# Twenty output units of the third layer as Strassen pairs over both halves, computed ahead of the merge, and a table builder that holds its two tiles

## The chip, the cores and the metric

One core of a Trainium2 chip runs the whole program: three layers of a sequence model, one launch. The metric is device time in microseconds (us). Engines: PE does matmuls, ACT, DVE and POOL elementwise work, and SP issues most of the DMAs. Each engine executes its own list of instructions in a fixed order; an instruction that must wait holds up all that stand behind it on that engine.

## The reference

Input x is 1024 tokens of width 1024. Two layers of a mixer and a gated feed-forward network come first, then one block of two branches:

```
x = first_block(x, ...)        # two layers, each a mixer and a gated FFN
xn = rmsnorm_2(h, norm_pre_g[l])
proj = xn @ w_in[l]
u_a, z_a, o_a, i_a, f_a, u_b, z_b, g_pre = jnp.split(proj, split_points, axis=-1)
y_a = mlstm_branch(u_a, z_a, o_a, i_a, f_a, ...) @ w_a_out[l]
y_b = s5_branch(u_b, z_b, ...) @ w_b_out[l]
g = jax.nn.sigmoid(g_pre.astype(jnp.float32)).astype(h.dtype)
merged = g[..., :D_MODEL] * y_a + g[..., D_MODEL:] * y_b
h = h + rmsnorm_2(merged @ w_o[l], norm_post_g[l])
```

z_b is 512 wide and g_pre 2048. In output units of 128 columns of `w_in`, z_b is units 28 to 31, the first gate (g1) units 32 to 39, the second (g2) units 40 to 47. The state-space branch (s5) also needs tables of powers of its complex coefficients, which depend on weights alone.

## The kernel before

The tokens are two halves h of 512 columns. Activations lie as tiles of 128 x 512, eight for the model width. A product in 32-bit precision is made of three matmuls per k tile, since each operand is split into a high and a low part: high by high, high by low, low by high (`mm3`, L236 to L238). Weights come as tiles `raw` (SP, L175) and are split by ACT (L186) and DVE (L188) into `wsp`. The feed-forward up-products are already done by Strassen's scheme over a pair of output units and both halves (`quad`, L497): seven half-depth products take the place of eight, each of 12 matmuls. The first product of a pair can be computed earlier on half 0 alone (`ffn_first`) and kept in DRAM.

Tiles come from pools with fixed slots: `t4` (27 slots, a split tile of 128 x 2 x 512), `t2` (18 slots, 128 x 512), `raw` (3), `wsp` (8). A tile holds its slot until its last use; the first instruction on the next tile of that slot waits for it. A scheduler fixes the order of each engine in advance. Side work runs as generators, advanced a little at each group of matmuls (`start(generator, rate)`) and finished by `drain`.

Two places matter here. In layer 0's FFN, the down-product (`ffn_down`, L630 to L632, output `pd`) of half 0 has the s5 table builder (`s5_tables`) beside it. The builder makes 16 tables in eight rounds of two on POOL: clear a tile `s5R` (L1315, L1316), double the powers eight times (L1323 to L1328, with a scratch tile `s5rt`), and write both tables by DMAs that POOL issues (L1332). Then `hid_steps(1)` fetches the 22 tiles `hidd1_k` from DRAM into `xt` (SP, L260) and splits them into `hid` (ACT L246, DVE L250), which the down-product of half 1 needs in the order of k.

At the end of the third layer the merge of a half takes the s5 branch's output `y` (POOL `y5n` L1769, split into `y5s`), multiplies it by the glu weights (`pgl`), fetches the other branch's output `oar` (POOL `oa` L1781, DVE L1782), and multiplies both into `pya` and `pyb`. Units z_b (`pzb`, `merge_z`), g1 (`pg1`, `merge_g`) and g2 (`pg2`) are computed within and ahead of each merge; `proj_out` (`po`) and `finish` (norm and residual) follow.

Of the kernel before, what the change touches and what calls it, by code (L numbers as in the profile page):

```python
# [11 lines left out]
F32 = mybir.dt.float32  # L12
# [3 lines left out]
AF = mybir.ActivationFunctionType  # L16
ALU = mybir.AluOpType
# [32 lines left out]
class Weights:  # L50
# [13 lines left out]
    def part(self, k0):  # L64
        return Weights(self.parts, self.q, self.k0 + k0)


class Model:
# [20 lines left out]
    bg = ()  # L89
# [227 lines left out]
            self.nc.tensor.transpose(pb[:, 128 * b:128 * b + 128], r[:, b:b + 1].to_broadcast([128, 128]), self.ident)  # L317
        return pb

    def norm_steps(self, h, gname, gi, out):  # L320

        nc = self.nc
        pb = self.bcast(self.r[h])
        for k, t in enumerate(self.fetch(self.x[h][:NT])):
            nc.vector.scalar_tensor_tensor(t, t, self.col(gname, gi * NT + k), pb, ALU.mult, ALU.mult)
            out.append(self.split(t, "xs", low=nc.vector if k % 2 else nc.gpsimd))
            yield

# [904 lines left out]
    def s5_tables(self):  # L1233
        nc, io = self.nc, self.io
# [26 lines left out]
        cs, sn = sm("cs"), sm("sn")  # L1261
# [48 lines left out]
        V.tensor_tensor(t0, t0, t1, ALU.subtract)  # L1310
        V.tensor_tensor(qi, t0, den, ALU.mult)
        yield
        for g0 in range(0, 16, 2):
            R = self.t4("s5R", [128, 2, 2, 256], F32)
            G.memset(R[:, :, 0, 0:1], 1.0)  # L1315
            G.memset(R[:, :, 1, 0:1], 0.0)  # L1316
            tp = self.t2("s5rt", [128, 2, 2, 128])
            for k in range(8):
                n = 1 << k
                er, ei = (E[k][i][:, g0:g0 + 2].unsqueeze(2).to_broadcast([128, 2, n]) for i in range(2))  # L1320
                s, d = slice(0, n), slice(n, 2 * n)
                tm = (tp[:, 0, :, :n], tp[:, 1, :, :n])
                G.tensor_tensor(tm[0], R[:, :, 0, s], er, ALU.mult)  # L1323
                G.tensor_tensor(tm[1], R[:, :, 1, s], ei, ALU.mult)
                G.tensor_tensor(R[:, :, 0, d], tm[0], tm[1], ALU.subtract)
                G.tensor_tensor(tm[0], R[:, :, 0, s], ei, ALU.mult)
                G.tensor_tensor(tm[1], R[:, :, 1, s], er, ALU.mult)
                G.tensor_tensor(R[:, :, 1, d], tm[0], tm[1], ALU.add)  # L1328
                if k > 2:
                    yield  # L1330
            for i in range(2):
                G.dma_start(self.s5r[g0 + i], R[:, i])  # L1332
            yield
# [411 lines left out]
            nc.sync.dma_start(self.oad[h][:, k], hn[i])  # L1745
            yield

    def merge_z(self, xs):

        out = []  # L1750
        for c in range(2):
            for sp in self.wpair(self.io["w2_in"], 14 + c):
                ps = self.ps("pzb")
                self.mm3(ps, sp, xs, bg=1)
                z = self.t2("zb")
                self.nc.scalar.activation(z, ps, AF.Tanh, scale=0.5)
                self.nc.vector.scalar_tensor_tensor(z, z, 1.0, ps, ALU.add, ALU.mult)
                out.append(z)
                self.etick()
        return out  # L1760

    def merge_y(self, h):

# [19 lines left out]
            oa.append(t)  # L1783
        return oa

    def merge_g(self, xs, c, bg):

        out = []
        for sp in self.wpair(self.io["w2_in"], 16 + c):
            ps = self.ps("pg1")  # L1790
            self.mm3(ps, sp, xs, bg=bg)
            out.append(self.t2("g1"))
            self.nc.scalar.activation(out[-1], ps, AF.Tanh, scale=0.5)
        return out

    def merge(self, xs, h, zb, y, g1=()):

        nc, io = self.nc, self.io
        V = nc.vector
        yn, ys = y  # L1800
        if h:
            self.drain()
            oa = self.merge_oa(h)
        yb = []
        for c in range(2):
            for i, sp in enumerate(self.wpair(io["w2_glu"], c)):
                k = 2 * c + i
                pg = self.pa("pgl")
                self.mm3(pg, sp, ys, bg=1)
                t = self.t2("glu")  # L1810
                nc.scalar.activation(t, pg, AF.Tanh, scale=0.5, bias=self.hbglu[:, k:k + 1])
                V.scalar_tensor_tensor(t, t, 1.0, yn[k], ALU.add, ALU.mult)
                V.tensor_tensor(t, t, zb[k], ALU.mult)
                yb.append(self.split(t, "yb", 0.125))
                self.etick()
        if not h:
            oa = self.merge_oa(h)
        out = []
        for c in range(4):
            pr = g1 if g1 and not c else self.merge_g(xs, c, 0.5)  # L1820
            for t, sp in zip(pr, self.wpair(io["w2_ao"], c)):
                pa = self.ps("pya")
                self.mm3(pa, sp, oa, bg=0.5)
                V.scalar_tensor_tensor(t, t, 1.0, pa, ALU.add, ALU.mult)
            w2, wb = self.wpair(io["w2_in"], 20 + c), self.wpair(io["w2_bo"], c)
            for i in range(2):
                ps = self.ps("pg2")
                self.mm3(ps, w2[i], xs, bg=0.5)
                t = self.t2("g2")
                nc.scalar.activation(t, ps, AF.Tanh, scale=0.5)  # L1830
# [10 lines left out]
    def block2(self, xsA, norm, dst):  # L1841

        io = self.io
        xs = [xsA, []]
        self.s5_in(xs[0], 0)
        self.xs_store(xs[0], 0)
        st = self.mconv(xs[0], 0, 0)
        g = self.start(self.mgates(xs[0], 0))
        self.mout(xs[0], 0, st)
        self.finished()  # L1850
        nb = self.start(norm(xs[1]), 3.0)
        self.mz(xs[0], 0, st)
        self.drain(nb)
        self.s5_in(xs[1], 1)
        self.xs_store(xs[1], 1)
        self.drain(g)
        self.start(self.s5_main(), 2.2)
        a = b = ()
        for h in range(NH):
            for hd in range(4):  # L1860
                units = 2 * ("o" not in st) + 2 * ("z" not in st) + 2 * (hd < 3 or h == 0) + 4 * (hd == 3 and h == 1)
                self.drain(a)
                a, b = b, self.start(self.mattn(h, hd, st), self.TH / units)
                new = None
                if "o" not in st:
                    self.mout(xs[h], hd, st)
                if hd < 3:
                    new = self.mconv(xs[h], h, hd + 1)
                if "z" not in st:
                    self.mz(xs[h], hd, st)  # L1870
                if hd == 3 and h == 0:
                    xs[1] = self.xs_load(1)
                    g = self.start(self.mgates(xs[1], 1))
                    new = self.mconv(xs[1], 1, 0)
                    self.drain(g)
                if hd == 3 and h:
                    zb = self.merge_z(xs[1])
                    y = self.merge_y(1)
                    g1 = self.merge_g(xs[1], 0, 1)
                st = new  # L1880
        self.ahead = 90
        mg = self.merge(xs[1], 1, zb, y, g1)
        xs[0] = self.xs_load(0)
        m, ss = self.proj_out(io["w2_o"], mg)
        self.finish(1, m, ss, "norm_post_g_2", 0, dst=dst(1))
        y = self.merge_y(0)
        zb = self.merge_z(xs[0])
        mg = self.merge(xs[0], 0, zb, y)
        m, ss = self.proj_out(io["w2_o"], mg, last=True)
        self.finished()  # L1890
        self.finish(0, m, ss, "norm_post_g_2", 0, dst=dst(0), last=True)
        self.finished()

    def run(self, out):
# [4 lines left out]

        B, keep = [{}, {}], [[self.dp.tile([128, T], F32, name=f"keep{l}_{k}") for k in range(NT)] for l in range(2)]  # L1900
        self.hidd = [[self.dp.tile([128, T], F32, name=f"hidd{h}_{j}") for j in range(FFT)] for h in range(NH)]
        self.m1d = [self.dp.tile([128, T], F32, name=f"m1d{j}") for j in range(FFT)]

        def side():
# [3 lines left out]
            self.drain(nb)  # L1908
            self.ffn_first(0, FFT - 14, B[0], None)

        def hook(gname, gi):
            def steps():
                xs[0] = []
                yield from self.norm_steps(0, gname, gi, xs[0])
            return steps

        self.ahead = 90
# [23 lines left out]
            self.finish(h, *self.proj_out(io["od_out"], y[h]), "mix_post_g", 1, rate=0.5 if h == 0 else 1.25, pool=h == 1)  # L1941
        self.drain(nb)
        self.ahead = 90
        self.ffn(1, B[1], keep[1], ("ffn_pre_g", 1), hook("norm_pre_g_2", 0), (self.s5_tables2(), 2.6), 7)
        self.ahead = 90
        self.block2(xs[0], lambda o: self.norm_steps(1, "norm_pre_g_2", 0, o), part(out))


@with_exitstack
# [63 lines left out]
```

## Time and profile before

| what | value |
|---|---|
| median of 3 runs | 3246.97 us (3246.46 to 3247.01) |
| the profiled execution | 3246.84 us |
| its span, first to last instruction | 3245.1 us |
| mean granted clock of PE | 0.985 |
| PE busy | 3120.8 us (96%), 14320 matmuls |
| DVE busy | 2279.1 us (70%) |
| ACT busy | 1511.6 us (47%) |
| POOL busy | 784.9 us (24%) |

The terms of this document's sums refer to the profiled execution. The granted clock is a share of PE's full speed of 2.4 GHz: 0.50 is 1.2 GHz. Matmuls overlap one another, so the spacing of their starts, not the duration of one, is what a matmul costs.

### The profile page before, as it was taken

What the parts mean: (1) busy time and instruction counts of PE and PEld (TensorE: products, weight loads), DVE (VectorE), ACT (ScalarE), POOL (GpSimd) and SP (SyncE); (2) the same over time, 40 slices, a digit from 0 to 9 for tenths busy, and PEclk for the clock granted to TensorE, in tenths of its full rate; (3) what the DMA queues carried; (4) which work ended last, traced back from release to release, by engine and by line L of the source; (5) the groups of instructions that cost most, each with busy time, mean ns of one, the idle gap of its engine ahead of it and who ended that gap; (6) DMA issues with size and microseconds to landing.
All of it is one profiled execution on the core that took longest, in us unless ns stands there. A gap on an engine that the chain in (4) does not pass through costs nothing. (4 is left out here: it accounts for less than half of the span.)

```text
span 3245.1 us, 42204 instructions
## 1 busy us (share of the span) xinstructions
PE 3120.8 (96%) x14320; PEld 2546.8 (78%) x14320; DVE 2279.1 (70%) x4391; ACT 1511.6 (47%) x2804; POOL 784.9 (24%) x992
## 2 busy tenths in 40 slices
PE   8999998999996998999999999999999999999998
PEld 5777786888885787877788888778887878888886
DVE  7768758568873569597756887777687988743633
ACT  4646644433432457575433345545454445333332
POOL 4111104455459302022535530001010100100200
PEclk9999999999998999999999999999999999999999
DMA  4444445233443644346423355657544444434532
GB/s 153 160 133 141 140 141 174 85 109 129 155 158 115 213 129 133 91 139 225 152 82 129 126 174 169 215 190 242 173 133 167 128 146 143 132 95 149 179 101 95
DMA packets 206154, 474.07 MB, mean 146 GB/s; under 512 B 25705, under 2 KB 48425, under 8 KB 205937
## 3 DMA queue, kind: packets, MB, share of 16 engines
q1 hardware_dynamic: 204656, 467.18, 43.7%
q0 software_dynamic: 1280, 4.20, 0.3%
q8 instruction: 113, 1.85, 0.2%
q14 instruction: 105, 0.85, 0.1%
HBM read 367.86 MB, written 99.19 MB: 144 GB/s over the span
## 5 line engine op out<-in xcount | busy, mean ns | idle before, releaser
L188 DVE TENSOR_TENSOR wsp<-raw,wsp 128x512 fp32r<-128x512 f32 x890 | 651.6, 738 | 447.2 <-ACT wsp L186 442.6
L186 ACT ACTIVATE wsp<-raw 128x512 fp32r<-128x512 f32 x882 | 541.0, 617 | 819.7 <-PE pd L632 180.5
L630 PE MATMUL pd<-hid,wsp 128*128 128x512 f32 x704 | 279.6, 398 | 30.6 <-ACT hid L246 30.6
L631 PE MATMUL pd<-hid,wsp 128*128 128x512 f32 x704 | 279.1, 397 | 4.1 <-DVE hid L250 4.0
L632 PE MATMUL pd<-hid,wsp 128*128 128x512 f32 x704 | 278.6, 396 | 0.0
L630 PEld LDWEIGHTS pd<-hid,wsp 128*128 128x128 f32 x704 | 134.4, 191 | 59.6 <-ACT hid L246 32.2
L631 PEld LDWEIGHTS pd<-hid,wsp 128*128 128x128 f32 x704 | 134.2, 191 | 37.1 <-DVE hid L250 9.6
L492 PE MATMUL qy<-st,wsp 128*128 128x512 f32 x416 | 162.2, 390 | 0.5 <-ACT qm L502 0.5
L493 PE MATMUL qy<-st,wsp 128*128 128x512 f32 x416 | 161.9, 389 | 0.0
L494 PE MATMUL qy<-st,wsp 128*128 128x512 f32 x416 | 161.9, 389 | 0.0
L236 PE MATMUL pg<-xs,wsp 128*128 128x512 f32 x384 | 150.9, 393 | 10.6 <-DVE l1h L725 6.3
L632 PEld LDWEIGHTS pd<-hid,wsp 128*128 128x128 f32 x704 | 134.5, 191 | 27.1
L248 POOL TENSOR_TENSOR xs<-xt,xs 128x512 fp32r<-128x512 f32 x28 | 44.3, 1584 | 456.7 <-ACT xs L246 401.6
L238 PE MATMUL pg<-xs,wsp 128*128 128x512 f32 x384 | 150.1, 391 | 0.0
L237 PE MATMUL pg<-xs,wsp 128*128 128x512 f32 x384 | 150.0, 391 | 0.0
L524 POOL TENSOR_TENSOR qv<-qv,qu 128x512 f32<-128x512 f32 x44 | 69.9, 1589 | 287.4 <-ACT wsp L186 137.2
L186 ACT ACTIVATE wsp<-wss 128x512 fp32r<-128x512 f32 x88 | 55.6, 632 | 150.4 <-PE qy L494 66.4
L270 DVE TENSOR_TENSOR sq<-sq 128x512 f32<-128x512 f32 x140 | 98.4, 704 | 32.3 <-ACT sq L268 31.8
L188 DVE TENSOR_TENSOR wsp<-wss,wsp 128x512 fp32r<-128x512 f32 x88 | 79.8, 907 | 28.7 <-ACT wsp L186 26.7
L492 PE MATMUL pf<-xs,wsp 128*128 128x512 f32 x224 | 89.5, 400 | 7.8 <-DVE th L577 5.2
L236 PEld LDWEIGHTS pg<-xs,wsp 128*128 128x128 f32 x384 | 72.5, 189 | 27.4 <-ACT yo L246 6.7
L492 PEld LDWEIGHTS qy<-st,wsp 128*128 128x128 f32 x416 | 78.1, 188 | 17.9 <-ACT qm L502 0.9
(716 smaller groups left out, 8904.4 us busy)
## 6 DMA issues: line engine op xcount, KB each, us to landing
raw<-in_w_in_dram SPq DMA_DIRECT2D x96, 512.0 KB
xt<-xres SPq DMA_DIRECT2D x128, 256.0 KB
raw<-in_wd_dram SPq DMA_DIRECT2D x64, 512.0 KB
raw<-in_wg_dram SPq DMA_DIRECT2D x58, 512.0 KB
raw<-in_wu_dram SPq DMA_DIRECT2D x58, 512.0 KB
hidd<-th SPq DMA_DIRECT2D x88, 256.0 KB
xt<-hidd SPq DMA_DIRECT2D x88, 256.0 KB
raw<-in_ev_in_dram SPq DMA_DIRECT2D x32, 512.0 KB
```

What stands on the lines that cost most here:

```text
L186: nc.scalar.activation(sp[:, 0], raw, AF.Copy)
L188: nc.vector.tensor_tensor(sp[:, 1], raw, f(sp[:, 0]), ALU.subtract)
L236: nc.tensor.matmul(ps, h, xs[k][:, 0], start=i == 0, stop=False)
L237: nc.tensor.matmul(ps, h, xs[k][:, 1], start=False, stop=False)
L238: nc.tensor.matmul(ps, l, xs[k][:, 0], start=False, stop=i == len(xs) - 1)
L270: nc.vector.tensor_tensor(q, q, acc, ALU.add)
L492: nc.tensor.matmul(ps, h, xs[k][:, 0], start=start and k == 0, stop=False, skip_group_check=not start)
L493: nc.tensor.matmul(ps, h, xs[k][:, 1], start=False, stop=False, skip_group_check=not start)
L494: nc.tensor.matmul(ps, l, xs[k][:, 0], start=False, stop=k == n - 1, skip_group_check=not start)
L630: nc.tensor.matmul(ps, h_, x[:, 0], start=k0 + k == 0, stop=False)
L631: nc.tensor.matmul(ps, h_, x[:, 1], start=False, stop=False)
L632: nc.tensor.matmul(ps, l_, x[:, 0], start=False, stop=k0 + k == FFT - 1)
```

## The change

Units 28 to 47 leave the merges. `late_firsts` computes the first Strassen product of each of the ten pairs, and the rest of the first unit's product, on half 0 before the quads begin, and keeps the product in DRAM (`m1l`). `late_rest` runs the other five products of each pair over both halves, and its sink stores tanh results in DRAM (`lated`). The merges load them again (`late`, tiles `lu`). For this, the normalised activations of both halves are stored (`kept`), fetched again, and their sums formed by `sum_steps`. The load of half 0's split activations (`xs_load(0)`) moves ahead of the firsts. The 960 matmuls of these units become 240 (`pl`) + 600 (five products of 12, ten pairs).

In `s5_tables`, the pair of tiles R and tp is taken once ahead of the loop over the rounds.

```
+        R = self.t4("s5R", [128, 2, 2, 256], F32)
+        tp = self.t2("s5rt", [128, 2, 2, 128])
         for g0 in range(0, 16, 2):
-            R = self.t4("s5R", [128, 2, 2, 256], F32)
             G.memset(R[:, :, 0, 0:1], 1.0)
             G.memset(R[:, :, 1, 0:1], 0.0)
-            tp = self.t2("s5rt", [128, 2, 2, 128])
...
+    def late_sink(self, c):
...
+            t = self.t2("lt")
+            nc.scalar.activation(t, a, AF.Tanh, scale=0.5)
+            if c < 32:
+                nc.vector.scalar_tensor_tensor(t, t, 1.0, a, ALU.add, ALU.mult)
+            self.store(self.lated[h][c + i], t)
+        return sink
+
+    def late_firsts(self, cs, xs):
...
+        for c in cs:
+            w.append(self.wtile(self.io["w2_in"][c]))
+            ps.append(self.ps("pl"))
+            self.prod(ps[-1], w[-1], xs[:4], True, 1)
+            m1 = self.t2("m1")
+            nc.scalar.activation(m1, ps[-1], AF.Copy)
+            self.store(self.m1l[c], m1)
+        for c, p, v in zip(cs, ps, w):
+            self.prod(p, v.part(4), xs[4:], False, 1)
+            self.late_sink(c)(0, 0, p, None)
+
+    def late_rest(self, c, B):
+        m1 = self.t2("m1")
+        self.flush()
+        self.nc.sync.dma_start(m1, self.m1l[c])
+        w = self.io["w2_in"]
+        self.quad(self.wquad(w[c], w[c + 1], True), B, self.late_sink(c), self.pa if c % 4 else self.ps, m1)
...
-    def merge(self, xs, h, zb, y, g1=()):
+    def merge(self, h, y):
...
+        zb = [self.late(28 + k, h) for k in range(4)]
...
-            pr = g1 if g1 and not c else self.merge_g(xs, c, 0.5)
+            pr = [self.late(32 + 2 * c + i, h) for i in range(2)]
...
+            g2 = [self.late(40 + 2 * c + i, h) for i in range(2)]
...
-                if hd == 3 and h:
-                    zb = self.merge_z(xs[1])
-                    y = self.merge_y(1)
-                    g1 = self.merge_g(xs[1], 0, 1)
...
+        x0 = self.xs_load(0)
+        B = {"b11": x0[:4], "b21": x0[4:]}
+        for c in range(28, 48, 4):
+            if c == 40:
+                self.drain()
+                got = self.fetch([self.kept[h][k + j] for k in range(NT // 2) for j in (0, NT // 2) for h in range(2)])
+                nb = self.start(self.sum_steps(lambda k, h: next(got), NT // 2, B), 2.5)
+            self.late_firsts((c, c + 2), x0)
+        self.drain(nb)
...
+        for c in range(28, 48, 2):
+            if c == 46:
+                y = self.merge_y(1)
+            self.late_rest(c, B)
...
-        mg = self.merge(xs[1], 1, zb, y, g1)
-        xs[0] = self.xs_load(0)
+        mg = self.merge(1, y)
...
         y = self.merge_y(0)
-        zb = self.merge_z(xs[0])
-        mg = self.merge(xs[0], 0, zb, y)
+        mg = self.merge(0, y)
```

SP's queue in layer 0's FFN, where it fetches `hidd1_4` to `hidd1_15` for the down-product of half 1; in brackets the semaphores an instruction waits for (`Pool` is a POOL instruction, `DMAHW` a DMA, `PE` and `DVE` those engines). Before:

```order
430 L260 DMA xt_9760<-hidd1_4_192 128x512 [waits Pool_49]
431 L260 DMA xt_9765<-hidd1_5_193 128x512 [waits DMAHW6_49]
432 L260 DMA xt_9770<-hidd1_6_194 128x512 [waits DMAHW7_49,Pool_49]
433 L260 DMA xt_9775<-hidd1_7_195 128x512 [waits DMAHW0_49]
434 L260 DMA xt_9780<-hidd1_8_196 128x512 [waits DMAHW1_49,Pool_49]
435 L260 DMA xt_9785<-hidd1_9_197 128x512 [waits DMAHW2_49,Pool_49]
436 L260 DMA xt_9790<-hidd1_10_198 128x512 [waits DMAHW3_49]
437 L260 DMA xt_9795<-hidd1_11_199 128x512 [waits DMAHW4_49,Pool_49]
438 L260 DMA xt_9800<-hidd1_12_200 128x512 [waits DMAHW5_49]
439 L260 DMA xt_9805<-hidd1_13_201 128x512 [waits DMAHW6_49,Pool_49]
440 L260 DMA xt_9810<-hidd1_14_202 128x512 [waits DMAHW7_49,Pool_49]
441 L260 DMA xt_9815<-hidd1_15_203 128x512 [waits DMAHW0_49,DVE_49]
```
After:
```order
430 L260 DMA xt_9814<-hidd1_4_192 128x512
431 L260 DMA xt_9819<-hidd1_5_193 128x512 [waits DMAHW6_49]
432 L260 DMA xt_9824<-hidd1_6_194 128x512 [waits DMAHW7_49]
433 L260 DMA xt_9829<-hidd1_7_195 128x512 [waits DMAHW0_49,PE_49]
434 L260 DMA xt_9834<-hidd1_8_196 128x512 [waits DMAHW1_49]
435 L260 DMA xt_9839<-hidd1_9_197 128x512 [waits DMAHW2_49]
436 L260 DMA xt_9844<-hidd1_10_198 128x512 [waits DMAHW3_49]
437 L260 DMA xt_9849<-hidd1_11_199 128x512 [waits DMAHW4_49]
438 L260 DMA xt_9854<-hidd1_12_200 128x512 [waits DMAHW5_49]
439 L260 DMA xt_9859<-hidd1_13_201 128x512 [waits DMAHW6_49]
440 L260 DMA xt_9864<-hidd1_14_202 128x512 [waits DMAHW7_49,Pool_49]
441 L260 DMA xt_9869<-hidd1_15_203 128x512 [waits DMAHW0_49,Pool_49]
```
Before, loads 4, 6, 8, 9, 11, 13 and 14 wait for POOL; after, only 14 and 15. Behind them stand loads 16 to 21 and then weight tiles of `wd`, in both. The POOL instructions that 14 and 15 wait for after are the last two of the builder, in its eighth round; before, 13 and 14 wait for the last of rounds six and seven.

POOL's list at the end of the builder's second round, with the two table writes and the clears of the next rounds (`DMASW` is a DMA that POOL issued). Before:
```order
355 L1328 TENSOR_TENSOR s5R_9123<-s5rt_9126 128x2x128 [waits Pool_49]
356 L1332 DMA s5r2_660<-s5R_9123 128x512 [waits Pool_49]
357 L1332 DMA s5r3_661<-s5R_9123 128x512
358 L1315 MEMSET s5R_9243 128x2 [waits DMASW1_49,DMASW0_49]
359 L1316 MEMSET s5R_9243 128x2
360 L1315 MEMSET s5R_9358 128x2 [waits DMASW3_49,DMASW2_49]
361 L1316 MEMSET s5R_9358 128x2
```
After:
```order
355 L1331 TENSOR_TENSOR s5R_9068<-s5rt_9069 128x2x128 [waits Pool_49]
356 L1335 DMA s5r2_726<-s5R_9068 128x512 [waits Pool_49]
357 L1335 DMA s5r3_727<-s5R_9068 128x512
358 L1319 MEMSET s5R_9068 128x2 [waits DMASW3_49,DMASW2_49]
359 L1320 MEMSET s5R_9068 128x2
360 L1326 TENSOR_TENSOR s5rt_9069<-s5R_9068,s5c_8507 128x2 [waits Pool_49]
```
Before, rounds three and four have a tile each, their clears stand together, and the two rounds then alternate step by step. After, each round clears the one tile and waits for both writes of the round ahead of it. (The builder's lines are numbered 3 or 4 higher after.)

PE's list between the projection of half 1 (`po`) and the glu product of half 0's merge (`pgl`), with the norm's small matmuls (`sst`, `rb`). Before:
```order
13047 L281 MATMUL sst_27342<-ones2_71,sq_27197 128x2 [waits PE_49]
13048 L236 MATMUL pzb_27363<-xs_26897,wsp_27313 128x512
13049 L281 MATMUL sst_27342<-ones2_71,sq_27197 128x2
13050 L237 MATMUL pzb_27363<-xs_26897,wsp_27313 128x512
13051 L281 MATMUL sst_27342<-ones2_71,sq_27197 128x2
13052 L238 MATMUL pzb_27363<-xs_26897,wsp_27313 128x512
13053 L281 MATMUL sst_27342<-ones2_71,sq_27197 128x2
13054 L236 MATMUL pzb_27363<-xs_26899,wsp_27313 128x512
13055 L237 MATMUL pzb_27363<-xs_26899,wsp_27313 128x512
13056 L238 MATMUL pzb_27363<-xs_26899,wsp_27313 128x512
13057 L236 MATMUL pgl_27416<-y5s_27204,wsp_27408 128x512 [waits Activation_49]
13058 L237 MATMUL pgl_27416<-y5s_27204,wsp_27408 128x512
```
After:
```order
13319 L238 MATMUL po_28178<-mrg_27913,wsp_28184 128x512
13320 L281 MATMUL sst_28325<-ones2_71,sq_28212 128x2 [waits DVE_49,PE_49]
13321 L281 MATMUL sst_28325<-ones2_71,sq_28212 128x2 x3
13322 L317 MATMUL rb_28363<-ident_66,nr_28331 128x128 [waits DVE_49,PE_49]
13323 L317 MATMUL rb_28363<-ident_66,nr_28331 128x128
13324 L236 MATMUL pgl_28261<-y5s_28219,wsp_28253 128x512 [waits Activation_49]
13325 L236 MATMUL pgl_28281<-y5s_28219,wsp_28258 128x512
13326 L236 MATMUL pgl_28311<-y5s_28219,wsp_28303 128x512
13327 L317 MATMUL rb_28363<-ident_66,nr_28331 128x128
13328 L237 MATMUL pgl_28261<-y5s_28219,wsp_28253 128x512 [waits DVE_49]
```
Before, 96 `pzb` matmuls stand there, of which the rows show the last; after, none, and `pgl` is the first long product after `po`.

## Rows read from the trace of the kernel before

**Rows 1.** The page, part 1: busy us, share of the span, instructions.
```profile
PE 3120.8 (96%) x14320; PEld 2546.8 (78%) x14320; DVE 2279.1 (70%) x4391; ACT 1511.6 (47%) x2804; POOL 784.9 (24%) x992
```

**Rows 2.** Timeline of PE, full stretch: start, duration, operation, count, [idle before, releaser].
```profile
2849.82 0.39 PE L238 MATMUL pg<-xs,wsp 128*128 128x512 f32 x1
...
2894.02 0.39 PE L238 MATMUL pya<-oa,wsp 128*128 128x512 f32 x1
```

**Rows 3.** Windows beside the builder: length, busy PE PEld DVE ACT POOL, clock, DMA, GB/s.
```profile
1000.00:1020.00 20.00, 14.36 (x64) 11.46 (x63) 10.06 (x23) 9.66 (x17) 17.38 (x50) 0.91 0.71 243
1020.00:1040.00 20.00, 11.61 (x43) 8.50 (x42) 9.65 (x13) 4.91 (x9) 15.88 (x69) 0.84 0.17 54
1040.00:1060.00 20.00, 2.02 (x3) 0.79 (x3) 2.07 (x2) 1.51 (x3) 19.17 (x51) 0.50 0.20 65
1060.00:1080.00 20.00, 19.68 (x80) 15.72 (x81) 13.25 (x20) 7.79 (x14) 17.88 (x42) 0.90 0.81 295
```

**Rows 4.** Waits of SP's queue at 980 to 1100 us: total, times, longest.
```profile
SPq L260 <- POOL s5R L1328: 39.7, 3, 27.8
```

**Rows 5.** Timeline of POOL, then of PE, where that wait ends.
```profile
1055.84 1.05 POOL L1328 TENSOR_TENSOR s5R<-s5rt 128x256 f32<-128x256 f32 x1
...
1060.32 0.79 PE L630 MATMUL pd<-hid,wsp 128*128 128x512 f32 x1 [2.73 <-ACT hid L246]
```

**Rows 6.** Timeline of POOL in the builder: table writes and tile clears.
```profile
941.92 1.31 POOL L1332 DMA_DIRECT2D s5r<-s5R  x2 [0.31 <-POOL s5R L1328]
...
963.77 1.14 POOL L1332 DMA_DIRECT2D s5r<-s5R  x2 [0.30 <-POOL s5R L1328]
...
968.90 0.10 POOL L1315 MEMSET s5R<- 128x2 f32 x1 [3.84 <-DMA s5r<-s5R]
...
1001.64 0.12 POOL L1315 MEMSET s5R<- 128x2 f32 x1
...
1023.80 1.15 POOL L1332 DMA_DIRECT2D s5r<-s5R  x2 [0.30 <-POOL s5R L1328]
1028.59 0.10 POOL L1315 MEMSET s5R<- 128x2 f32 x1 [3.64 <-DMA s5r<-s5R]
...
1057.19 1.12 POOL L1332 DMA_DIRECT2D s5r<-s5R  x2 [0.30 <-POOL s5R L1328]
```

**Rows 7.** Two of the builder's multiplications on POOL, same shape.
```profile
1017.98 1.13 POOL L1324 TENSOR_TENSOR s5rt<-s5R,s5c 128x256 f32<-128x256 f32 x1
...
1050.24 0.65 POOL L1327 TENSOR_TENSOR s5rt<-s5R,s5c 128x256 f32<-128x256 f32 x1
```

**Rows 8.** Windows, same columns, where the Strassen products of layers 0 and 1 begin.
```profile
520.00:540.00 20.00, 17.97 (x78) 14.25 (x77) 18.28 (x22) 9.15 (x17) 11.70 (x8) 1.00 0.63 221
540.00:560.00 20.00, 12.28 (x40) 9.12 (x39) 14.10 (x14) 7.25 (x13) 12.59 (x9) 0.74 0.04 16
1560.00:1580.00 20.00, 17.58 (x76) 13.65 (x74) 17.61 (x18) 8.74 (x16) 16.05 (x10) 1.00 0.62 218
1580.00:1600.00 20.00, 18.12 (x71) 14.51 (x72) 18.18 (x22) 11.24 (x20) 13.82 (x9) 0.91 0.30 106
```

**Rows 9.** Window, same columns, of the third layer's end.
```profile
3020.00:3040.00 20.00, 20.00 (x91) 16.33 (x91) 19.09 (x36) 10.03 (x17) 7.09 (x2) 1.00 0.65 223
```

**Rows 10.** Timeline of POOL and DVE ahead of half 0's merge.
```profile
2998.09 1.36 POOL L1769 TENSOR_SCALAR y5n<-y 128x512 f32<-128x512 f32 x1 [185.34 <-DMA y<-yd]
...
3010.49 0.68 DVE L250 SCALAR_TENSOR_TENSOR y5s<-y5n,y5s 128x512 fp32r<-128x512 f32 x1
```

**Rows 11.** Groups by line, 2990 to 3060 us: busy, mean ns, idle before.
```profile
L1781 POOL TENSOR_SCALAR oa<-oar 128x512 fp32r<-128x512 f32 x8 | 14.0, 1770 | 23.3 <-DMA oar<-oad 23.3
```

**Rows 12.** DMA issues at 2700 to 3000 us: queue, operation, count, KB each.
```profile
xs<-xsd SPq DMA_DIRECT2D x8, 512.0 KB
```

More of the change, by code (lines that the diff above doesn't have):

```diff
@@ L318, in bcast, with norm_steps @@
         return pb
-    def norm_steps(self, h, gname, gi, out):
+    def norm_steps(self, h, gname, gi, out, keep=None):
         nc = self.nc
@@ L325, in norm_steps @@
             nc.vector.scalar_tensor_tensor(t, t, self.col(gname, gi * NT + k), pb, ALU.mult, ALU.mult)
+            if keep:
+                self.store(keep[k], t)
             out.append(self.split(t, "xs", low=nc.vector if k % 2 else nc.gpsimd))
@@ L1746, in mattn, with sink, late @@
             yield
[L1748 to L1760, printed above, removed]
+    def late_sink(self, c):
+        nc = self.nc
+        def sink(i, h, a, b):
+            if b is not None:
+                t = self.t2("qt")
+                nc.vector.tensor_tensor(t, a, b, ALU.add)
+                a = t
+            t = self.t2("lt")
[5 more added lines that the diff above has]
+    def late_firsts(self, cs, xs):
+        nc = self.nc
+        ps, w = [], []
+        for c in cs:
[14 more added lines that the diff above has]
+        self.quad(self.wquad(w[c], w[c + 1], True), B, self.late_sink(c), self.pa if c % 4 else self.ps, m1)
+    def late(self, c, h):
+        t = self.t2("lu")
+        self.nc.sync.dma_start(t, self.lated[h][c])
+        return t
     def merge_y(self, h):
@@ L1784, in merge_oa @@
         return oa
[L1786 to L1794, printed above, removed]
-    def merge(self, xs, h, zb, y, g1=()):
+    def merge(self, h, y):
         nc, io = self.nc, self.io
@@ L1800, in merge @@
         yn, ys = y
+        zb = [self.late(28 + k, h) for k in range(4)]
         if h:
-            self.drain()
             oa = self.merge_oa(h)
@@ L1824, in merge @@
                 V.scalar_tensor_tensor(t, t, 1.0, pa, ALU.add, ALU.mult)
[L1825 to L1830, printed above, removed]
+            wb = self.wpair(io["w2_bo"], c)
+            g2 = [self.late(40 + 2 * c + i, h) for i in range(2)]
+            for i, t in enumerate(g2):
                 pb = self.ps("pyb")
@@ L1860, in block2 @@
             for hd in range(4):
-                units = 2 * ("o" not in st) + 2 * ("z" not in st) + 2 * (hd < 3 or h == 0) + 4 * (hd == 3 and h == 1)
+                units = 2 * ("o" not in st) + 2 * ("z" not in st) + 2 * (hd < 3 or h == 0) + 10 * (hd == 3 and h == 1)
                 self.drain(a)
@@ L1875, in block2 @@
                     self.drain(g)
-                if hd == 3 and h:
-                    zb = self.merge_z(xs[1])
-                    y = self.merge_y(1)
-                    g1 = self.merge_g(xs[1], 0, 1)
                 st = new
+        x0 = self.xs_load(0)
[7 more added lines that the diff above has]
+        self.drain(nb)
+        self.ahead = 150
+        for c in range(28, 48, 2):
+            if c == 46:
+                y = self.merge_y(1)
+            self.late_rest(c, B)
         self.ahead = 90
-        mg = self.merge(xs[1], 1, zb, y, g1)
-        xs[0] = self.xs_load(0)
+        mg = self.merge(1, y)
         m, ss = self.proj_out(io["w2_o"], mg)
@@ L1901, in run @@
         self.hidd = [[self.dp.tile([128, T], F32, name=f"hidd{h}_{j}") for j in range(FFT)] for h in range(NH)]
+        self.kept = [[self.dp.tile([128, T], F32, name=f"kept{h}_{k}") for k in range(NT)] for h in range(NH)]
+        self.lated = [{c: self.dp.tile([128, T], F32, name=f"lated{h}_{c}") for c in range(28, 48)} for h in range(NH)]
+        self.m1l = {c: self.dp.tile([128, T], F32, name=f"m1l{c}") for c in range(28, 48, 2)}
         self.m1d = [self.dp.tile([128, T], F32, name=f"m1d{j}") for j in range(FFT)]
@@ L1909, in side, with hook @@
             self.ffn_first(0, FFT - 14, B[0], None)
-        def hook(gname, gi):
+        def hook(gname, gi, keep=None):
             def steps():
                 xs[0] = []
-                yield from self.norm_steps(0, gname, gi, xs[0])
+                yield from self.norm_steps(0, gname, gi, xs[0], keep)
             return steps
@@ L1943, in run @@
         self.ahead = 90
-        self.ffn(1, B[1], keep[1], ("ffn_pre_g", 1), hook("norm_pre_g_2", 0), (self.s5_tables2(), 2.6), 7)
+        self.ffn(1, B[1], keep[1], ("ffn_pre_g", 1), hook("norm_pre_g_2", 0, self.kept[0]), (self.s5_tables2(), 2.6), 7)
         self.ahead = 90
-        self.block2(xs[0], lambda o: self.norm_steps(1, "norm_pre_g_2", 0, o), part(out))
+        self.block2(xs[0], lambda o: self.norm_steps(1, "norm_pre_g_2", 0, o, self.kept[1]), part(out))
 @with_exitstack
```

## The prediction

> **What bounds the kernel now.** I read the totals first: TensorE is busy 3120.8 us of a span of 3245.1 [rows 1]; the profiled execution took 3246.84 us, 1.7 us around its span and 0.13 under the median of the runs shown. So the end moves with the number of matmuls and with the places where PE stands still. Then the price of a matmul: in a full stretch 195 starts lie 44.20 us apart, 0.2267 us each [rows 2]. Then the windows, for the places where PE is not full. The largest is beside the table builder of layer 0: from 1000 to 1080 us it ran 190 matmuls, 43.1 us of work, so 36.9 us are lost, at granted clocks down to 0.50 (that is 1.2 GHz; it idles there, then comes back) [rows 3]. The waits of SP's queue name what ends it: loads of `hidd` for half 1 stand behind the builder's last operation of a round, 39.7 us in three waits, the longest 27.8 [rows 4]. Those loads take tile slots that the builder held; POOL frees one at 1056.89 and PE goes on at 1060.32, 3.4 us later [rows 5]. In the third layer's end PE is full, and other engines have work to spare except near 3030 us, where DVE is busy 19.09 of 20 [rows 9].
>
> **A. The held tiles: +48 us.** The instruction order settles what happens to the slots. Before, seven of the first 16 `hidd1` loads wait for POOL, because each builder round gives its pair of tiles back; after, only `hidd1_14` and `hidd1_15` do. One pair is now held through all eight rounds, so the last use of either tile is in the eighth round, and these two loads wait for that round's last operations, not for round six or seven. SP's queue is in order: behind `hidd1_14` stand six more `hidd1` loads and the weight tiles of `wd`. PE computes the first down-product up to k = 13 (42 matmuls) and then needs `hid` number 14. So the question is when round eight ends.
>
> Before, two rounds could run interleaved on two pairs. After, every round clears the same tile that two DMAs have just read out of, and the clear waits for both to land. Where the trace shows this (a clear right behind the writes of its own tile) it cost 3.84 and 3.64 us, mean 3.74 [rows 6]; issuing two table writes takes POOL 1.15. Every further round thus pays 4.89 outside its arithmetic. The arithmetic: 20.5 us from the end of one issue (943.23) to the next (963.77) and 22.2 from the clear at 1001.64 to 1023.80, both single rounds while DVE works; an interleaved pair with DVE nearly idle took 28.6 for two, 14.3 each [rows 6]. One multiplication of the same shape took 1.13 us in the first setting and 0.65 in the second [rows 7]. In the new order the three rounds after the first fall before PE stops, DVE working: 20.5 each. The last four fall into the stall, where DVE runs dry (2.07 of 20 [rows 3]); I take 17, nearer to 14.3 than to 22.2, because a single round has no second chain to fill the gaps between its dependent steps. The first round is unchanged and begins its writes at 941.92. Round eight ends at 941.92 + 7 × 4.89 + 3 × 20.5 + 4 × 17 = 1105.6, less the 0.3 between last operation and issue: 1105.3. With the same 3.4 to PE it goes on at 1108.7 in place of 1060.32: **+48.4**. Nothing covers it, since PE's queue is in order too; what follows is what followed before. Bounds: all rounds at 14.3, ending at 1076, +19; all at 22.2, ending at 1131, +75.
>
> The Trainium skill speaks against holding one tile: "Trainium Kernel Development and Optimization", section Best Practices, says to double-buffer so that DMA overlaps compute. The two waits of 3.84 and 3.64 us agree; by the rule alone, 7 × 3.74 = 26 us of such waits would be added in place of 48, which is rival R3. The same notes ("SBUF — State Buffer", section SBUF: two separate sides) say that VectorE and GpSimd share a port pair as an exclusive lock. The 1.13 against 0.65 fits that; by the rule the stalled rounds should be the quick ones, as taken here.
>
> **B. Fewer products: −27.2 us.** Twenty output units on two halves were 20 × 2 × 24 = 960 matmuls. Now ten firsts of 24 and ten quads of five products of 12: 840. At full rate 120 × 0.2267 = 27.2.
>
> **C. What the third layer's end loses: +34 us.** Before, the z_b and g units were spread between the merge's dependent steps and gave PE work while tiles were fetched. They leave the merge.
> C1, before the merge of half 0: 96 `pzb` matmuls (21.8 us) stood between the last `po` and the first `pgl`; after, PE goes from `po` to `pgl` with only the norm's small matmuls in between. From the first `y5n` to the last `y5s` took 2998.09 to 3011.17, 13.1 us [rows 10]; the eight `oa` conversions took 14.0 on POOL behind their loads [rows 11]; the 48 `pgl` matmuls cover 10.9. In series: 13.1 + 14.0 − 10.9 = 16. If the first part hides under `po`: 3. If the loads also meet the DVE backlog of that time [rows 9]: some 7 more, 24. I take 16.
> C2, before the merge of half 1: the same chain, with a last quad (60 matmuls, 13.6 us) beside it: 16 − 13.6, about 3; bounds 0 and 16.
> C3, the start of the quads: their sums of activations are made by DVE and POOL shortly ahead. The same start cost 40 − 118 × 0.2267 = 13.2 us in layer 0 and 40 − 147 × 0.2267 = 6.7 in layer 1 [rows 8]. Here 96 matmuls cover it, but the sums also wait for 16 loads: 10, bounds 0 and 13.
> C4, half 0's activations come back by eight loads of 512 KB [rows 12], now ahead of the firsts and not beside a projection. At the 295 GB/s of the best window [rows 3] that is 14 us; most lies beside the last head's products: 5, bounds 0 and 14.
> The added instructions on ACT, DVE and POOL (30, 52, 64) and 122 DMAs lie beside full matmul stretches where these engines have room, and cost nothing there; at the one crowded place they are in C1's bound.
>
> **Sum.** 3246.84 + 48.4 − 27.2 + 34 = **3302 us**, 1.7% slower. About 0.2%, 6.5 us, is what a measurement here tells from no change.
>
> **Rivals.**
> R1, the end hides its fetches: C1 at 3, C2 0, C3 6.7, C4 0, so about 10 in place of 34: 3278. For it: SP has slack in the last 200 us, and loads that wait for no slot can run ahead. Against: the `y5` loads stand behind weight loads whose tiles come free only as splits go on. Chance 0.22.
> R2, DVE stays busy in the stall and all later rounds take 22.2: +75, with C at 34: 3329. Against it the 2.07 of 20. Chance 0.13.
> R3, the rounds keep the pace they had, and only the waits of seven clears are added: 7 × 3.74 = 26 in place of 48: 3280. For it: before, too, DVE's work and not the pairing set much of a round's length. Against it: the interleaved pairs were the quick rounds. Chance 0.06. (This is what the double-buffering rule of the Trainium skill, by itself, would give.)
> R4, the other side: the held pair gives the loads their slots and the builder is early enough. That takes round eight to end before PE reaches k = 14. SP began these loads at about 1009 before, and PE needs 9.5 us for 42 matmuls, so the end must lie near 1018: (1018 − 941.92 − 34.2) / 7 = 6 us of arithmetic for a round, below half of the quickest seen. Then the 36.9 us of [rows 3] go: 3246.84 − 36.9 − 27.2 + 34 = 3217, faster. Chance 0.04, mostly for an error of mine in which operation frees the slot.
> R5, hold and new stalls together equal the 27 us saved (A at 19, C at 8): 3247, same. Chance 0.03.
> The forecast, 3285 to 3320, has the remaining 0.52. Range for 8 in 10: 3264 to 3334, from below R1 and R3 to R2 above. Slower by over 0.2%: 0.93; within: 0.03; faster: 0.04.
>
> **What would show it.** For A: SP's one long wait at `hidd1_14` for POOL, ending near 1105; PE nearly idle from about 1020 to 1108 at clock 0.50; seven clears of 3.7 us wait on POOL. A release near 1060 or before would refute it. For B: 120 matmuls fewer, and stretches of quads without gaps. For C: idle PE ahead of the first `pgl` of half 0 released by `y5s`, then ahead of `pya` released by `oa`; ahead of the first quad, released by a split. If PE is full there, C falls and R1 holds. The prediction is wrong as a whole if the builder's rounds shorten a lot or the late loads issue far ahead.

## The result and the profile after

The changed kernel takes 3323.4 us (median of four runs, 3319.5 to 3328.3) against 3247.0 (3246.5 to 3251.7): ratio 1.0233, interval 1.0215 to 1.0251. The forecast was 3302, range 3264 to 3334. Its profiled execution took 3319.48 us, 72.6 more than the one of before, and the losses below are counted in it.

The windows beside the table builder (columns as in [rows 3], to which they answer) and, under them, those of three places in the third layer:

```profile
1000.00:1020.00 20.00, 14.46 (x65) 11.52 (x64) 9.18 (x22) 7.57 (x14) 15.69 (x40) 0.91 0.69 230
1020.00:1040.00 20.00, 12.50 (x46) 9.21 (x45) 8.71 (x14) 6.07 (x11) 14.50 (x44) 0.84 0.13 50
1040.00:1060.00 20.00, 0.00 (x0) 0.00 (x0) 0.00 (x0) 0.00 (x0) 15.11 (x53) 0.50 0.07 27
1060.00:1080.00 20.00, 0.00 (x0) 0.00 (x0) 0.00 (x0) 0.00 (x0) 15.15 (x53) 0.50 0.06 26
1080.00:1100.00 20.00, 0.00 (x0) 0.00 (x0) 0.00 (x0) 0.00 (x0) 15.14 (x53) 0.50 0.07 27
1100.00:1120.00 20.00, 13.12 (x46) 10.03 (x47) 8.30 (x13) 8.89 (x15) 5.17 (x9) 0.70 0.77 276
2860.00:2880.00 20.00, 13.66 (x51) 9.85 (x50) 15.10 (x15) 10.70 (x20) 13.24 (x9) 0.92 0.78 293
2880.00:2900.00 20.00, 13.86 (x48) 9.67 (x47) 14.13 (x15) 8.36 (x15) 15.30 (x11) 0.82 0.30 105
2900.00:2920.00 20.00, 19.68 (x87) 15.95 (x87) 16.51 (x19) 6.99 (x12) 14.75 (x10) 1.00 0.33 107
3020.00:3040.00 20.00, 15.12 (x55) 11.98 (x54) 8.90 (x12) 7.02 (x13) 5.58 (x5) 0.83 0.39 119
3040.00:3060.00 20.00, 17.75 (x69) 13.52 (x69) 14.82 (x20) 8.17 (x15) 7.10 (x8) 0.91 0.93 330
3160.00:3180.00 20.00, 14.21 (x56) 10.64 (x55) 12.11 (x28) 6.01 (x11) 6.18 (x6) 0.83 0.58 199
3180.00:3200.00 20.00, 12.60 (x45) 9.28 (x45) 19.49 (x30) 6.10 (x11) 13.44 (x6) 0.83 0.74 262
```

From 1040 to 1100 us every engine but POOL stands still: not one instruction on PE, DVE or ACT. At the first quads PE runs 186 matmuls in 60 us, so 60 − 186 × 0.2267 = 17.8 are lost; at the merge of half 1 124 in 40, 11.9 lost; at the merge of half 0 101 in 40, 17.1 lost (a few small matmuls of the norm are among them).

What ends the long stall, in the waits of SP's queue from 980 to 1160 us, POOL's timeline and PE's (these answer to [rows 4] and [rows 5]):

```profile
SPq L260 <- POOL s5rt L1330: 86.0, 1, 86.0
```

```profile
1103.63 0.72 POOL L1331 TENSOR_TENSOR s5R<-s5rt 128x256 f32<-128x256 f32 x1
1104.65 1.13 POOL L1335 DMA_DIRECT2D s5r<-s5R  x2 [0.30 <-POOL s5R L1331]
...
1106.88 0.79 PE L632 MATMUL pd<-hid,wsp 128*128 128x512 f32 x1 [74.39 <-ACT hid L246]
```

One wait of 86.0 us in place of three of 39.7, and PE goes on at 1106.88 where it did at 1060.32 before: 46.6 later.

### The profile page after: what moved, and what is told of

Read it like the earlier page. It is cut to its first block, busy times and chain, and to the rows that moved or that the text cites. A ratio compares the mean times of both kernels' runs of the same rounds, so it can differ in the third digit from the quotient of the medians.

```text
span 3317.8 us, 42390 instructions
## 1 busy us (share of the span) xinstructions
PE 3112.0 (94%) x14200; PEld 2532.0 (76%) x14200; DVE 2329.5 (70%) x4443; ACT 1527.5 (46%) x2834; POOL 876.8 (26%) x1056
## 5 line engine op out<-in xcount | busy, mean ns | idle before, releaser
L188 DVE TENSOR_TENSOR wsp<-raw,wsp 128x512 fp32r<-128x512 f32 x850 | 631.0, 748 | 373.5 <-ACT wsp L186 368.5
L186 ACT ACTIVATE wsp<-raw 128x512 fp32r<-128x512 f32 x842 | 515.5, 616 | 743.7 <-PE pd L634 199.0
L494 PE MATMUL qy<-st,wsp 128*128 128x512 f32 x496 | 194.7, 393 | 6.0 <-ACT lt L1762 5.2
L495 PE MATMUL qy<-st,wsp 128*128 128x512 f32 x496 | 193.8, 391 | 0.7 <-DVE st L248 0.7
L496 PE MATMUL qy<-st,wsp 128*128 128x512 f32 x496 | 193.5, 390 | 0.0
L526 POOL TENSOR_TENSOR qv<-qv,qu 128x512 f32<-128x512 f32 x54 | 87.6, 1622 | 334.4 <-ACT wsp L186 189.7
L186 ACT ACTIVATE wsp<-wss 128x512 fp32r<-128x512 f32 x108 | 68.2, 631 | 183.3 <-PE qz L496 77.6
L250 DVE SCALAR_TENSOR_TENSOR hid<-xt,hid 128x512 fp32r<-128x512 f32 x88 | 57.8, 687 | 83.3 <-ACT hid L246 83.1
L188 DVE TENSOR_TENSOR wsp<-wss,wsp 128x512 fp32r<-128x512 f32 x108 | 95.6, 886 | 29.0 <-ACT wsp L186 26.0
L494 PEld LDWEIGHTS qy<-st,wsp 128*128 128x128 f32 x496 | 93.6, 189 | 27.7 <-ACT lt L1762 5.6
L495 PEld LDWEIGHTS qy<-st,wsp 128*128 128x128 f32 x496 | 93.5, 189 | 20.1 <-DVE st L248 1.1
L496 PEld LDWEIGHTS qy<-st,wsp 128*128 128x128 f32 x496 | 93.5, 189 | 19.6
L210 POOL TENSOR_TENSOR wss<-raw 128x512 f32<-128x512 f32 x54 | 75.2, 1393 | 97.5 <-DMA raw<-in_w_in_dram 40.5
```

Of the source, the lines that this page charges most:

```text
L186: nc.scalar.activation(sp[:, 0], raw, AF.Copy)
L188: nc.vector.tensor_tensor(sp[:, 1], raw, f(sp[:, 0]), ALU.subtract)
L210: G.tensor_tensor(t[:, lo], r1[:, lo], r1[:, hi], ALU.add)
L494: nc.tensor.matmul(ps, h, xs[k][:, 0], start=start and k == 0, stop=False, skip_group_check=not start)
L495: nc.tensor.matmul(ps, h, xs[k][:, 1], start=False, stop=False, skip_group_check=not start)
L496: nc.tensor.matmul(ps, l, xs[k][:, 0], start=False, stop=k == n - 1, skip_group_check=not start)
```

## The experiments

Ratios are to runs of the kernel before on the same chip, whose median lay at 3251.1 for e1 to e4, 3250.2 for e5 to e8 and 3250.3 for e9.

**e1, the held tiles alone.** The kernel before with

```
+        R = self.t4("s5R", [128, 2, 2, 256], F32)
+        tp = self.t2("s5rt", [128, 2, 2, 128])
         for g0 in range(0, 16, 2):
-            R = self.t4("s5R", [128, 2, 2, 256], F32)
...
-            tp = self.t2("s5rt", [128, 2, 2, 128])
```

> The kernel before with the held pair of builder tiles alone. Theory A (the two loads wait for the eighth round): the release moves from 1060.3 to about 1107.6 us as in the changed kernel, +47, so 3294, and PE stands still from about 1035 to 1107. Rival (only the waits of the clears are added): +26 at most, 3273. Rival (the hold costs nothing and the whole loss is in the third layer): 3247.

3297.1 us, ratio 1.0148 (1.0133 to 1.0163): 46 more. Its PE timeline has the same row at the same place:

```profile
1107.11 0.80 PE L630 MATMUL pd<-hid,wsp 128*128 128x512 f32 x1 [73.08 <-ACT hid L246]
```

The theory's 47; both rivals (3273 and 3247) fall.

**e2, the third layer alone.** The changed kernel with the two tiles taken in each round, as before (e1's diff the other way round).

> The changed kernel with the builder of before. Theory B + C (27.2 us saved, some 47 lost in three new stalls of the third layer's end, a few more lost on the way): 3272 to 3277, the stalls near 2815 (first quads), 2975 (merge of half 1) and 3115 (merge of half 0) with about 18, 12 and 17 us. Rival (the stalls of the end follow from the hold, through a shift of the order): 3220, without them.

3270.6 us, ratio 1.0068 (1.0052 to 1.0085): 19.5 more. The three stalls are there without the hold. In its windows of 20 us, 181 matmuls from 2800 to 2860, 127 from 2960 to 3000 and 190 from 3100 to 3160: 19.0, 11.2 and 16.9 us lost, 47.1 in all. Less the 27.2 saved that is 19.9, against 19.3 between the two spans. The third layer's part is accounted for. The rival is refuted. The two ratios together, 1.0148 × 1.0068 = 1.0217, come near the 1.0233 of the whole change.

**e3, a builder that holds no slot of the loads.** The changed kernel with

```
-        E = [(sm(f"er{k}"), sm(f"ei{k}")) for k in range(8)]
+        et = self.small("s5e", [128, 16, 16], bufs=1)
+        E = [(et[:, 2 * k], et[:, 2 * k + 1]) for k in range(8)]
...
-        R = self.t4("s5R", [128, 2, 2, 256], F32)
-        tp = self.t2("s5rt", [128, 2, 2, 128])
+        for t, d in zip(big, self.s5c):
+            nc.sync.dma_start(d, t)
+        R = self.p.tile([128, 2, 2, 256], F32, tag="wss", bufs=1, name="s5R")
+        tp = self.p.tile([128, 2, 2, 128], F32, tag="ws1", bufs=1, name="s5rt")
...
-        for t, d in zip(big, self.s5c):
-            nc.sync.dma_start(d, t)
```

> The changed kernel, but the held builder pair lies in the two weight-sum tiles that are idle at that time, the coefficients lie in a small tile of their own, and the other constants are stored ahead of the rounds: no load of hidd waits for the builder, whose rounds stay single and keep the waits of their clears. Theory A (the slot's release is the cost): the whole stall goes, 47 and the 37 of before, so 3323 - 84 = about 3239. Rival (the slower builder itself holds up others through POOL's queue): not under 3276, with a wait on POOL ahead of the next mixer's activations.

3244.6 us, ratio 0.9984 (0.9974 to 0.9994): 79 less than the changed kernel. The builder is slower than in that kernel, its last write begins at 1130.05 in place of 1104.65, but no wait of SP's queue from 980 to 1160 us names POOL any more. The stall is down to two windows, 138 matmuls in 40 us, 8.7 lost:

```profile
1000.00:1020.00 20.00, 14.79 (x63) 11.74 (x61) 8.16 (x20) 7.45 (x14) 16.86 (x47) 0.85 0.68 238
1020.00:1040.00 20.00, 20.00 (x75) 15.10 (x76) 15.71 (x26) 11.29 (x21) 12.69 (x28) 0.89 0.66 236
```

That a rest of 8.7 us stays was not foreseen. PE's timeline names its waits, and neither is for the builder:

```profile
1014.79 1.84 PE L281 MATMUL sst<-ones,sq 128*128 128x2 f32 x8 [3.04 <-DVE sq L270]
1019.86 0.80 PE L633 MATMUL pd<-hid,wsp 128*128 128x512 f32 x1 [2.17 <-DVE hid L250]
```

The two make 5.2 of the 8.7; beside and behind them, from 1014 to 1024 us, the granted clock is 0.50 to 0.52 (1.2 GHz), and matmuls there cost more. The kernel before has the same two waits at the same place, 2.72 and 2.92 us: that part of its 36.9 was not the builder's slots. So the builder's length, which is greater here than before and in the changed kernel, holds up no load; what costs is which instruction waits for it. Whether POOL's work makes DVE late for these two waits was not separated.

**e4, the fetches of the third layer earlier.** The kernel of e3 with the following, and 6 in place of 10 in the last head's `units`:

```
         mg = self.merge(1, y)
+        y = self.merge_y(0)
+        oa = self.merge_oa(0)
         m, ss = self.proj_out(io["w2_o"], mg)
...
-            if c == 40:
+            if c == 32:
...
-                nb = self.start(self.sum_steps(lambda k, h: next(got), NT // 2, B), 2.5)
+                nb = self.start(self.sum_steps(lambda k, h: next(got), NT // 2, B), 1.25)
```

> The kernel of e3, and two changes in the third layer's end: the y and oa loads and conversions of half 0 are placed ahead of the projection of half 1, and the sums for the quads start at the second group of firsts at half the rate. Theory C (fetches in series without cover): the merge stall of 17 us falls to about 4 and the quad stall of 18 to about 7, so 24 us less than e3, about 3215. Rival (tile slots or DVE bound these stages whatever the order): within 6 us of e3, about 3239.

3220.5 us, ratio 0.9909 (0.9895 to 0.9924): 24 less than e3, as expected. Its windows at the first quads, at the merge of half 1 and at that of half 0:

```profile
2780.00:2800.00 20.00, 16.79 (x73) 13.58 (x74) 17.65 (x15) 12.24 (x23) 15.99 (x11) 1.00 0.67 226
2800.00:2820.00 20.00, 17.26 (x68) 13.45 (x66) 17.20 (x15) 10.18 (x20) 16.95 (x11) 0.91 0.50 182
2820.00:2840.00 20.00, 18.78 (x81) 15.23 (x82) 17.50 (x20) 7.80 (x14) 14.76 (x9) 1.00 0.35 107
2940.00:2960.00 20.00, 15.22 (x60) 11.80 (x59) 8.87 (x13) 6.92 (x12) 4.64 (x4) 0.91 0.54 168
2960.00:2980.00 20.00, 17.45 (x68) 13.31 (x67) 13.29 (x18) 6.88 (x12) 9.00 (x9) 0.91 0.88 295
3080.00:3100.00 20.00, 20.00 (x94) 16.66 (x93) 14.18 (x30) 10.10 (x18) 0.00 (x0) 1.00 0.83 264
3100.00:3120.00 20.00, 20.00 (x91) 16.36 (x90) 19.57 (x34) 5.69 (x9) 0.00 (x0) 1.00 0.83 273
```

PE is full at the merge of half 0: 17 us gone, although DVE is as busy there as before (19.57 of 20). At the quads 222 matmuls in 60 us, 9.7 lost in place of 17.8. At the merge of half 1, where nothing was changed, 11.0 stay.

**e5, the same builder in the kernel before.**

> The kernel before, with the builder of e3 (own tiles, held, no slot of the loads) and nothing else. Theory A (the slot release is the cost, for the kernel before too): its stall of 37 us shrinks as in e3, where about 9 us stayed, so some 28 less than before, 3220. Rival (the pool of e3 only repaired what the new order broke): within 6 us of before.

3222.1 us, ratio 0.9918 (0.9902 to 0.9935): 28 less. The kernel before lost time to this slot, too, and the whole of the gain over it that e4 shows can be had without one Strassen pair.

**e6, the merge of half 1 earlier.** The kernel of e4 with `merge_y(1)` at c == 44 and, at c == 46, `oa = self.merge_oa(1, range(4))`, the other four in the merge.

> The kernel of e4, and for the merge of half 1 the y fetch stands one quad earlier and the first four oa fetches and conversions stand ahead of the last quad. Theory C (the fetch in series is the cost, about 11 us there): some 8 us less than e4, 3212. Rival (the 27 slots are full of the quads' sums, so that the fetches wait anyway, or now hold up the quads): within 3 us of e4, 3220, or above.

3220.3 us, ratio 0.9909 (0.9891 to 0.9928), the same as e4: the rival's number. Some 10 us are lost there still (219 matmuls from 2920 to 2980), and one wait in them is new: a first matmul of `pya` now stands in PE's list ahead of the last quad's end and waits for its `oa` tile, with the quad behind it.

```profile
2943.78 0.80 PE L236 MATMUL pya<-oa,wsp 128*128 128x512 f32 x1 [3.70 <-POOL oa L1815]
```

**e7, two held pairs in turn.** The changed kernel with `RT = [(self.t4(...), self.t2(...)) for _ in range(2)]` ahead of the loop and `R, tp = RT[g0 // 2 % 2]` in it.

> The changed kernel with two held pairs of builder tiles, used in turn. If the waits of the clears for the table writes (seven, 2.1 to 5.4 us, 23 in all) are a term of the stall of their own, they go and round eight ends some 23 us earlier: 3300, with PE idle until about 1084. Rival (POOL's pace alone sets it, the waits hid other delays): 3323 unchanged. Second rival (with two pairs the rounds interleave as before and the release falls back to round six or seven): 3276.

3313.0 us, ratio 1.0196 (1.0177 to 1.0214): 10 less, between the theory's 23 and the rival's nothing. The builder did end 25.4 us earlier (POOL's last table write begins at 1079.26 in place of 1104.65). The clears waited 10.8 us in all where they had waited 23.0, so 12.2 of the 25.4 are their waits. The rest has other causes: the rounds interleave again, and DVE did nothing from 1000 to 1040 us (0.00 of 20 in both windows), a setting in which POOL's operations were quick before [rows 7]. So the price of the waits alone is not shown by this run. And a second pair held is a second slot kept from others, and now another instruction waits for one. The waits of that kernel from 990 to 1100 us:

```profile
ACT m L636 <- DMA s5r<-s5R: 46.8, 1, 46.8
PE sst L281 <- DVE sq L270: 40.4, 1, 40.4
```

ACT's copy of half 0's down-product needed the tile and stood 46.8 us in ACT's queue, with all later weight splits behind it. Most of the early end was lost to that: from 1000 to 1120 us PE ran 201 matmuls where the changed kernel ran 156, 10.2 us of work more. The rule to double-buffer (the Trainium skill, "Trainium Kernel Development and Optimization", section Best Practices) agrees with the waits of the clears, 12.2 us fewer. The kernel gained only 10, since the second buffer was taken from slots that others wait for.

**e8, e4's first edit alone.**

> The kernel of e3 with the fetches for the merge of half 0 ahead of the projection of half 1, and the sums where the change has them. Theory C with separate terms: 17 us less than e3, 3228, the stall of the first quads unchanged at 18 us. Rival (the two terms share a cause, the DVE backlog): 24 less or under 8 less.

3226.8 us, ratio 0.9926 (0.9905 to 0.9947), 18 less than e3, with the quads' stall as it was (261 matmuls in the 80 us from 2780, 20.8 lost). The two terms are separate; the runs of this kernel spread over 13 us.

**e9, the sums beside all firsts.** The kernel of e6 with the sums begun at c == 28 at rate 1.0, the `drain()` there moved behind the firsts, and `units` back at 10.

> The kernel of e6, with the sums for the quads spread over all five groups of firsts (they begin with the first group, at four fifths of the rate) and the last head's work no longer finished ahead of them. Theory C3 (the sums' chain on DVE and POOL has too little cover): the 10 us that stay lost at the first quads fall to about 3, so 3213. Rival (DVE and POOL are full there, with the sums of weights for the first quads beside them, so spreading gains nothing): 3220. Second rival (the sums now hold slots that the last head needs): over 3225.

3220.6 us, ratio 0.9911 (0.9894 to 0.9927): nothing gained. The loss at the first quads fell to 4.2 us (158 matmuls in the 40 us from 2780), and a new window with 81 matmuls (2740 to 2760) ahead of it loses 1.6; e6 lost 9.9 at its quads (221 matmuls in the 60 us from 2760). So by the windows some 4 us were saved that the time does not show; the runs of e6 spread over 10 us. The time is the first rival's, and DVE is busy 18.14 and 18.73 of 20 at the quads, which fits its reason (no room on DVE) but does not show it.

## Why the forecast came out, point by point

**A, the held tiles: right in mechanism and size.** 48.4 forecast, 46.6 in the trace, 46 in e1. Round eight's last write begins at 1104.65; the sum gave 1105.6. Two of its parts were off and nearly cancelled, so that it came within 1 us is partly luck: the waits and issues took 31.2 us, not 34.2, and the seven rounds 131.4, not 129.5. The builder's clears, in POOL's timeline of the changed kernel:

```profile
947.74 0.10 POOL L1319 MEMSET s5R<- 128x2 f32 x1 [4.32 <-DMA s5r<-s5R]
...
996.82 0.10 POOL L1319 MEMSET s5R<- 128x2 f32 x1 [3.37 <-DMA s5r<-s5R]
...
1023.34 0.10 POOL L1319 MEMSET s5R<- 128x2 f32 x1 [5.38 <-DMA s5r<-s5R]
...
1044.68 1.15 POOL L1335 DMA_DIRECT2D s5r<-s5R  x2 [0.30 <-POOL s5R L1331]
1047.95 0.10 POOL L1319 MEMSET s5R<- 128x2 f32 x1 [2.12 <-DMA s5r<-s5R]
...
1064.70 1.14 POOL L1335 DMA_DIRECT2D s5r<-s5R  x2 [0.30 <-POOL s5R L1331]
1067.91 0.10 POOL L1319 MEMSET s5R<- 128x2 f32 x1 [2.07 <-DMA s5r<-s5R]
```

The wait is 3.4 to 5.4 us while PE and its fetches run and 2.1 in the stall, not 3.74 throughout. A round in the stall takes 16.8 from clear to write (1047.95 to 1064.70), 17 forecast; one of the earlier ones, 1023.34 to 1044.68, took 21.3; it began while DVE was still at work (8.71 of 20 in the window from 1020). R2 (22.2 throughout) is refuted by these rows, R3 (only the waits added) and R4 (the stall vanishes) by e1. R4 asked for rounds of 6 us; what removes the stall is not a quicker builder but a builder in other tiles (e3).

**B, 27.2 us saved: holds within the accounts.** PE has 120 instructions fewer (14200 for 14320) and the long stretches are full; e2's stalls less 27.2 give its time to 0.6 us.

**C, 34 forecast, 47 measured: the step that was too small.** By its terms: C1, the merge of half 0, 16 against 17.1. C3 and C4, the quads' start with the loads, 15 against 17.8 (the two were not told apart). C2, the merge of half 1, 3 against 11.9: this one failed. I had taken the last quad's 13.6 us off the chain as cover. The chain does lie beside it, but in the same queues. PE stops inside that quad, in the timelines of ACT and PE of the changed kernel:

```profile
3025.27 0.63 ACT L246 ACTIVATE y5s<-y5n 128x512 fp32r<-128x512 f32 x1 [3.71 <-POOL y5n L1802]
...
3027.20 0.58 ACT L504 ACTIVATE qv<-qz 128x512 f32<-128x512 f32 x1
...
3027.84 0.80 PE L494 MATMUL qz<-b,wsp 128*128 128x512 f32 x1 [4.88 <-ACT qv L504]
```

ACT waits for the `y5n` tiles in order, and the copy `qv` that the quad needs for its next product stands behind them. The cover itself was held up by what it was to cover. That is 4.88 of the 11.9 us; 2.25 more are a wait of `pya` for `oa` at 3046.76, and most of the rest lies behind these two, where PE goes on slowly: from 3028 to 3033 us it ran 12 matmuls, 0.43 us apart, at a granted clock of 0.50 (1.2 GHz). C2 had no term for what PE loses behind a wait. In e6, with `y5` fetched a quad earlier, the last quad has no such wait for `qv`, but the wait for `oa` has come into the quad, and the loss stays at some 10 us.

The same pattern stands at the first quads, in the timelines of ACT and PE:

```profile
2886.86 0.63 ACT L246 ACTIVATE st<-xt 128x512 fp32r<-128x512 f32 x1 [7.79 <-DVE xt L478]
...
2888.96 0.57 ACT L1762 ACTIVATE lt<-pl 128x512 f32<-128x512 f32 x1
...
2889.58 0.80 PE L494 MATMUL qy<-st,wsp 128*128 128x512 f32 x1 [5.20 <-ACT lt L1762]
```

The longest wait of PE there is not for a split, as forecast, but for the tanh of a finished `pl` product, which stood in ACT's queue behind a split that waited 7.79 us for its sum from DVE. And C1's size hides another composition. PE's waits at the merge of half 0:

```profile
3163.20 1.57 PE L281 MATMUL sst<-ones,sq 128*128 128x2 f32 x8 [2.63 <-DVE sq L270]
3167.10 0.66 PE L317 MATMUL rb<-ident,nr 128*128 128x128 f32 x2 [2.32 <-DVE nr L310]
3172.75 0.50 PE L237 MATMUL pgl<-y5s,wsp 128*128 128x512 f32 x1 [0.74 <-DVE y5s L250]
3190.34 0.80 PE L237 MATMUL pya<-oa,wsp 128*128 128x512 f32 x1 [7.32 <-DVE oa L1815]
```

The wait for `oa` is as forecast; the one for `y5s` is only 0.74, and 4.95 us are the norm's small matmuls, which had `pzb` between them before and had no price in the sum. That 16 came near 17.1 is in part luck.

The rival R1, that the end hides its fetches, is refuted by e2, and e4 shows that for one of the three places it was only a matter of the order.

**Left open.** 46.6 − 27.2 + 46.8 = 66.2 of the 72.6 between the two profiled executions. The forecast's sum was 55.2, 17.4 short of them: C was 12.8 too small, A 1.8 too large, and 6.4 stay unaccounted. The measured time lies in the range by the range's width, not by the sum. Of the 6.4, 4.5 lie between the first `pxr` matmul of layer 1, which comes 47.2 us later than before, and the first `mpn` matmul of the third layer, 51.7 later. No single wait was found for that. In e1 and in e2 the same stretch is 1.3 longer than before, so neither the hold nor the third layer's part shows it alone; four runs of the changed kernel spread over 9 us. The spans of e1 and of the kernel before differ by 50.3 where its stall gives 46.8, but against the runs of the kernel before that were taken with it e1's median differs by 46. In e2 the sum closes to 0.6. The net worth of the Strassen pairs with the fetches moved is below what these runs resolve: e4 and e5 differ by 1.6 us.

## What to carry to other kernels

A tile held over a loop gives its slot back at the loop's last use, whoever waits for it; what that costs is found in the instruction that takes the slot next and in the queue behind it, not in the time of the loop. When products are moved away, ask what they covered, and whether the next cover shares a queue with the fetch it is meant to hide: an in-order engine that waits for the fetch stops the cover, too. And before a saving of 27 us is built, look at whether a stall of 37 already stands in the profile: e5 took as much from that alone.

## What the runs showed of the hardware that was not expected

The clear behind the same two table writes waited 2.1 us in the stall and up to 5.4 us elsewhere in the changed kernel, 6.6 in e3. In windows of 4 to 8 us laid around six of these waits the DMA share was 0.32 (wait 2.12), 0.52 (3.37), 0.65 (3.64), 0.86 (4.32), 0.81 (5.38) and, in e3, 1.03 (6.58): a factor of three in one wait, and the longer ones where the DMA engines are busier. PE and DVE worked in all but the first, so whether the DMAs of others or DVE's work made the difference was not separated.

A round of the builder also has no fixed length. In e3 the round between these two rows takes 28.2 us, with DVE busy 15.71 and 17.41 of 20 in its two windows; the same operations took 16.8 in the stall of the changed kernel, with DVE at 0.00.

```profile
1026.01 0.10 POOL L1322 MEMSET s5R<- 128x2 f32 x1 [6.58 <-DMA s5r<-s5R]
...
1054.25 1.15 POOL L1338 DMA_DIRECT2D s5r<-s5R  x2 [0.30 <-POOL s5R L1334]
```

PE, ACT and the DMAs were busy there, too, so the runs do not show that DVE alone made the difference.
